# A hybrid decoder block on one core: new source for norm 1, RoPE on another engine, other orders of the split products

## The chip, the core and the metric

The kernel runs on one core of one Trainium2 chip. Its time is the device time of one execution in microseconds (us). Three runs of the kernel before took 1512.32, 1514.86 and 1514.89 us; the median is 1514.86 us. The engines are TensorE (PE in the profile; its weight loads are PEld), VectorE (DVE), ScalarE (ACT), GpSimd (POOL) and SyncE (SP), which here only issues DMAs.

## The reference

One decoder layer on x of 256 tokens x 2048 features, all in fp32. Two token mixers stand side by side and are merged by sigmoid gates; a SwiGLU FFN and a last norm follow. D_FF is 5632.

```
def rms_norm(x, w):
    y = xf * lax.rsqrt(jnp.mean(xf * xf, axis=-1, keepdims=True) + NORM_EPS)
    return (y * w.astype(jnp.float32)).astype(x.dtype)
...
def apply_rope(x, cos, sin):
    return jnp.concatenate([x1 * c - x2 * s, x2 * c + x1 * s], axis=-1).astype(x.dtype)
...
        h = rms_norm(x, norm1_w[l])
        proj = h @ w_in[l]
        nsa_q, nsa_kv, nsa_g, dn_qkv, dn_z, dn_a, dn_b, merge_g = jnp.split(proj, split_points(), axis=-1)
...
        mixed = g_nsa * (o_nsa @ w_up_nsa[l]) + g_dn * (o_dn @ w_up_dn[l])
        x = x + mixed @ w_o[l]
        h2 = rms_norm(x, norm2_w[l])
        x = x + (jax.nn.silu(h2 @ w_ffn_gate[l]) * (h2 @ w_ffn_up[l])) @ w_ffn_down[l]
    return rms_norm(x, norm_f_w)
```

## The kernel before, in words

Every weight matrix is streamed once through SBUF in tiles `raw` of 128 partitions x 2048 fp32 (1 MB; 708 KB in the first stage), three buffers deep, by SP's queue (`load`, L122). TensorE multiplies in fp32r, so each operand is cut in two parts: `split` (L133) lets ScalarE copy half a tile to `hi` (L141) and VectorE subtract it to get `lo` (L142), three buffers of each. A product of weight w and activation a is the sum of hi*hi, hi*lo and lo*hi. There are two ways to form it:

- `group` with `nat_mm` (L144, L234): the activation is the stationary operand and the weight streams, three products of up to 512 columns (L238 to L240). Used for the first stage (z, a, b and NSA gates, three groups of 354 to 356 columns, called zab), for v of NSA, for w_o and for the FFN's down projection.
- `group_t` (L180) and `group_s` (L206): the weight is stationary, the activation streams. `group_t` streams the activation's two parts at once (512 columns, L196) against w's hi, then the activation's hi (256 columns, L197) against w's lo; hi*hi and hi*lo land in two halves of a PSUM bank, which ScalarE and VectorE add afterwards (L200, L202). One such unit (weight tile k, column half f) is two products, and f is the innermost loop but the products of one unit stand together. `group_s` makes three products of 256 columns into one accumulator (L220 to L222), both f in one bank; it serves the DeltaNet's q, k and v (called wdn).

The stages follow each other on TensorE: zab, wdn (6 x 2 groups), NSA kv and q (`nsaT`) and v, merge gates (16 groups), DeltaNet's and NSA's up projections (`odn`, `onsa`), w_o, FFN gate and up (22 steps of two groups, `wfg`), FFN down. All small work of the mixers (conv, triangular solve, DeltaNet's chunk steps, RoPE, attention) is written as generators in three lanes; `pump` lets one step of each lane into the program after every half tile, so that this work lies between the products. The scheduler puts the splits some way ahead (`high_priority`), and instructions in `pin` keep their written order.

At the start, class `First` (L987) loads x transposed (`xT`), makes the hi and lo parts of x times the norm's weight (L1001, L1002), and lets GpSimd square and add the columns of `xT` (L1008, L1011, L1012). After the first group, `rms1` (L1050) sums these over the partitions by 8 fp32 products with a vector of ones (L1056, `ssx`) and takes the reciprocal root; the factor is applied when products leave PSUM. `rope` (L684) is four GpSimd instructions on each of three k tensors and four q tensors (L690 to L693): two on 64 partitions, two on 128, each of 512 elements. `solve` inverts a 32x32 triangle in 31 steps on VectorE, with a yield after most of them.

Of the kernel before, what the change touches and what calls it, by code (L numbers as in the profile page):

```python
# [14 lines left out]
P = 128  # L15
# [78 lines left out]
class Kern:  # L94
# [27 lines left out]
    def load(self, src, w, nk=4, parts=1):  # L122
# [3 lines left out]
        m = nk // parts  # L126
        for i in range(parts):
            nc.sync.dma_start(rv[:, i * m:(i + 1) * m, :], src[:, i * m:(i + 1) * m, :])
            if parts > 1:
                self.on_load(i)  # L130
        return rv

# [12 lines left out]
    def group(self, srcs, acts, w=512, first=None, t_outer=False):  # L145
# [3 lines left out]
        if t_outer:  # L149
            ps = [self.aux("mm")[:], self.aux("mm")[:]]  # L150
        else:
            bank = self.pmain.tile([P, 2, 512], F32, tag="mm", name=self.nm("mm"))
            ps = [bank[:, t, :] for t in range(2)]
        n = len(srcs)
        tail = []
        for c, src in enumerate(srcs):
            if first:
                first.load(c)
            rv = self.load(src, w, parts=2 if first and c == 0 else 1)
            for h in range(2):  # L160
                if first:
                    first.prep(c, h)
                hv, lv = self.split(rv, w, h)
# [16 lines left out]
    def group_t(self, srcs, acts, out=None):  # L180


        nc = self.nc
        ps = self.pmain.tile([P, 2, 2, 256], F32, tag="mm", name=self.nm("mm"))
        n = len(srcs)
        for c, src in enumerate(srcs):
            rv = self.load(src, 256, nk=8)
            for h in range(2):
                hv, lv = self.split(rv, 256, h)
                for k in range(4):  # L190
                    a = acts(c * 8 + h * 4 + k)
                    begin = c == 0 and h == 0 and k == 0
                    last = c == n - 1 and h == 1 and k == 3
                    for f in range(2):
                        fs = slice(f * P, f * P + P)
                        nc.tensor.matmul(ps[:, f], hv[:, k, fs], a, start=begin, stop=False, skip_group_check=True)  # L196
                        nc.tensor.matmul(ps[:, f, 0, :], lv[:, k, fs], a[:, 0, :], start=False, stop=last, skip_group_check=True)  # L197
                self.pump()
        e = self.wp.tile([P, 2, 256], F32, tag="ev", bufs=1, name=self.nm("ev"))
# [4 lines left out]

    def group_s(self, srcs, acts):

        nc = self.nc
        ps = self.pmain.tile([P, 2, 256], F32, tag="mm", name=self.nm("mm"))
        n = len(srcs)
        for c, src in enumerate(srcs):  # L210
            rv = self.load(src, 256, nk=8)
            for h in range(2):
                hv, lv = self.split(rv, 256, h)
                for k in range(4):
                    a = acts(c * 8 + h * 4 + k)
                    begin = c == 0 and h == 0 and k == 0
                    last = c == n - 1 and h == 1 and k == 3
                    for f in range(2):
                        fs = slice(f * P, f * P + P)
                        nc.tensor.matmul(ps[:, f], hv[:, k, fs], a[:, 0, :], start=begin and f == 0, stop=False, skip_group_check=True)  # L220
                        nc.tensor.matmul(ps[:, f], hv[:, k, fs], a[:, 1, :], start=False, stop=False, skip_group_check=True)  # L221
                        nc.tensor.matmul(ps[:, f], lv[:, k, fs], a[:, 0, :], start=False, stop=last, skip_group_check=True)  # L222
                self.pump()
        return ps[:]
# [202 lines left out]
    def solve(self):  # L427
# [28 lines left out]
        for q in range(4):  # L456
            self.pin(V.tensor_tensor(self.MT[:, 4 * q:4 * q + 4, :], self.MT[:, 4 * q:4 * q + 4, :],
                                     self.cs["offmask"][:, None, :].to_broadcast([P, 4, 128]), op=OP.mult))
            yield
# [3 lines left out]
        for j in range(31):  # L463
# [5 lines left out]
            if j % 2 or 7 < j < 23:  # L469
                yield  # L470
# [213 lines left out]
    def rope(self, x):  # L684

        G = self.nc.gpsimd
# [7 lines left out]
        t.free()  # L694

    def nsa_kv(self):
# [17 lines left out]
        nc.gpsimd.tensor_tensor(vc.ap, vc.ap, self.R[:, None, :].to_broadcast([P, 2, 256]), op=OP.mult)  # L714
        for x in (kc, ks, kw):
            self.rope(x)
            yield
# [68 lines left out]
    def nsa_q(self):  # L786
# [10 lines left out]
        for x in self.qT4:  # L797
            self.rope(x)
            yield
# [83 lines left out]
        def values(t, h, pt):  # L883
# [4 lines left out]
            for br in range(2):  # L888
                for kb in range(nb):
                    c = br * 256 + kvh * 128  # L890
                    nc.tensor.matmul(ov[:, j, :], self.vn[:, kb, c:c + 128], pt[:, br * nb + kb, :],  # L891
# [38 lines left out]
        self.vn.free()  # L930


    def build(self):
# [24 lines left out]
        nc.sync.dma_start(n1[:], t["n1"])  # L958

# [21 lines left out]
        acc = self.ar.alloc([4, 256], "y")  # L981
# [4 lines left out]
        class First:  # L986
# [6 lines left out]
            def part(_, h):  # L993
                nc.sync.dma_start(xT[:, 2 * h:2 * h + 2, :], t["xT"][:, 2 * h:2 * h + 2, :])

            def prep(_, c, h):
# [6 lines left out]
                if h:  # L1003
                    sq = self.ar.alloc([4, 256], "ym")
                    sqs.append(sq)
                    xc = xT[:, 4 * c:4 * c + 4, :]
                    if c < 3:
                        nc.gpsimd.tensor_tensor(sq.ap, xc, xc, op=OP.mult)  # L1008
                    else:
                        nc.scalar.activation(sq.ap, xc, AF.Square)  # L1010
# [337 lines left out]
```

## Time and profile before

| What | Value |
|---|---|
| Median of three runs | 1514.86 us |
| Profiled execution, its own time | 1514.85 us |
| Its span | 1513.1 us |
| PE busy | 1485.2 us (98%) |
| DVE, ACT, POOL busy | 971.9, 719.7, 147.6 us |
| Mean granted TensorE clock | 0.994 of 2.4 GHz |

The span runs from the first to the last instruction of the execution; 1.75 us of the execution's time lie around it. A busy PE does not say how fast it goes: its matmuls overlap, so the pace is read from starts, or from the number of matmuls in a stretch. Where PE waits, the waits and the order of time tell for whom.

### The profile page before, as it was taken

The numbers are of one execution on the slowest core, as the hardware profiler recorded it, in microseconds if no ns is written. First come the engines' busy times: TensorE is split into PE (matmuls) and PEld (weight loads), VectorE is DVE, ScalarE is ACT, GpSimd is POOL, SyncE is SP. The second block draws the span as 40 slices with busy tenths as digits, with TensorE's granted clock in tenths as the row PEclk, the third lists the DMA queues.
The fourth block names the chain that finished last, engine by engine and source line by source line (L and its number), as shares of the span: only waits on it lengthen the run. The fifth ranks groups of instructions, "written<-read, shape, count | busy, mean of one in ns | idle before, by whom it ended". The sixth has DMA issues, their size and how long they took to land.

```text
span 1513.1 us, 21295 instructions
## 1 busy us (share of the span) xinstructions
PE 1485.2 (98%) x8583; PEld 1303.0 (86%) x8583; DVE 971.9 (64%) x1400; ACT 719.7 (48%) x923; POOL 147.6 (10%) x109
## 2 busy tenths in 40 slices
PE   6999999999999999999999999999999999999997
PEld 6999998897888988888888888888888888888885
DVE  7679997668777765675665565555555555445443
ACT  5655444344455545554454444444445444333343
POOL 5000103302400000030000000000000000000000
PEclk9999999999999999999999999999999999999999
DMA  6654556345554465555455555555555556555553
GB/s 232 224 188 168 182 168 199 108 151 185 198 180 152 139 200 190 172 191 194 167 192 185 184 191 195 195 188 183 190 191 195 194 181 212 191 195 183 183 190 112
DMA packets 40947, 276.80 MB, mean 183 GB/s; under 512 B 4992, under 2 KB 5008, under 8 KB 9232
## 3 DMA queue, kind: packets, MB, share of 16 engines
q1 hardware_dynamic: 38592, 268.34, 52.3%
q10 hardware_dynamic: 1152, 4.46, 0.9%
q0 software_dynamic: 1104, 2.64, 0.7%
q8 instruction: 67, 1.10, 0.3%
q14 instruction: 32, 0.26, 0.0%
HBM read 272.52 MB, written 2.89 MB: 182 GB/s over the span
## 4 chain that ended last, share of the span: by engine, by line
PE 95%; DVE 3%; DMA 0%; issue 0%; ACT 0%; SPq 0%; DVEq 0%; ACTq 0%
PE mm L196 36%; PE mm L197 18%; PE mm L239 9%; PE mm L240 9%; PE mm L238 9%; PE mm L221 3%; PE mm L222 3%; PE mm L220 3%; DVE lo L142 1%; PE oacc L891 1%; PE U L563 1%; DMA raw<-in_zab 0%; PE pt L877 0%; DVE xs L468 0%; DVE main L376 0%
## 5 line engine op out<-in xcount | busy, mean ns | idle before, releaser
L142 DVE TENSOR_TENSOR lo<-raw,hi 128x1024 fp32r<-128x1024 f32 (+2 forms) x512 | 635.1, 1242 | 471.4 <-ACT hi L141 470.0
L141 ACT ACTIVATE hi<-raw 128x1024 fp32r<-128x1024 f32 (+2 forms) x512 | 535.6, 1047 | 728.3 <-PE mm L196 378.5
L196 PE MATMUL mm<-h,hi 128*128 128x512 f32 x1408 | 488.6, 392 | 0.0
L197 PE MATMUL mm<-h,lo 128*128 128x256 f32 x1408 | 394.6, 280 | 0.0
L196 PEld LDWEIGHTS mm<-h,hi 128*128 128x128 f32 x1408 | 264.2, 188 | 59.1
L196 PE MATMUL mm<-hh,hi 128*128 128x512 f32 x768 | 276.5, 401 | 0.0
L197 PEld LDWEIGHTS mm<-h,lo 128*128 128x128 f32 x1408 | 264.7, 188 | 0.0
L197 PE MATMUL mm<-hh,lo 128*128 128x256 f32 x768 | 217.5, 283 | 5.3 <-DVE lo L142 5.3
L196 PEld LDWEIGHTS mm<-hh,hi 128*128 128x128 f32 x768 | 145.1, 189 | 33.4 <-issue 0.2
L197 PEld LDWEIGHTS mm<-hh,lo 128*128 128x128 f32 x768 | 145.7, 190 | 7.4 <-DVE lo L142 7.2
L220 PE MATMUL mm<-hh,hi 128*128 128x256 f32 x384 | 108.7, 283 | 0.0
L221 PE MATMUL mm<-hh,hi 128*128 128x256 f32 x384 | 107.9, 281 | 0.0
L222 PE MATMUL mm<-hh,lo 128*128 128x256 f32 x384 | 107.9, 281 | 0.0
L1196 POOL TENSOR_TENSOR sgt<-sgt,R 128x512 f32<-128x512 f32 x22 | 39.6, 1802 | 536.9 <-ACT sgt L1195 536.9
L239 PE MATMUL mm<-lo,fxy 128*128 128x512 f32 x192 | 75.9, 395 | 0.0
L240 PE MATMUL mm<-hi,fxy 128*128 128x512 f32 x192 | 75.9, 395 | 0.0
L238 PE MATMUL mm<-hi,fxy 128*128 128x512 f32 x192 | 75.9, 395 | 0.0
L220 PEld LDWEIGHTS mm<-hh,hi 128*128 128x128 f32 x384 | 72.4, 188 | 0.0
L221 PEld LDWEIGHTS mm<-hh,hi 128*128 128x128 f32 x384 | 72.4, 189 | 0.0
L222 PEld LDWEIGHTS mm<-hh,lo 128*128 128x128 f32 x384 | 72.4, 188 | 0.0
L239 PE MATMUL mm<-lo,fa 128*128 128x512 f32 x160 | 63.2, 395 | 0.0
L238 PE MATMUL mm<-hi,fa 128*128 128x512 f32 x160 | 63.2, 395 | 0.0
(351 smaller groups left out, 1885.8 us busy)
## 6 DMA issues: line engine op xcount, KB each, us to landing
raw<-in_wfg SPq DMA_DIRECT2D x88, 1024.0 KB, 4.8
raw<-in_wd SPq DMA_DIRECT2D x44, 1024.0 KB, 4.8
raw<-in_wmg SPq DMA_DIRECT2D x32, 1024.0 KB, 4.8
raw<-in_wdn SPq DMA_DIRECT2D x24, 1024.0 KB, 4.9
raw<-in_nsa SPq DMA_DIRECT2D x16, 1024.0 KB, 4.8
raw<-in_wo SPq DMA_DIRECT2D x16, 1024.0 KB, 4.8
raw<-in_wud SPq DMA_DIRECT2D x8, 1024.0 KB, 4.9
raw<-in_wun SPq DMA_DIRECT2D x8, 1024.0 KB, 4.8
```

Source lines behind the costliest of these rows:

```text
L141: nc.scalar.activation(hv, rv[:, m * h:m * h + m, :], AF.Copy)
L142: nc.vector.tensor_tensor(lv, rv[:, m * h:m * h + m, :], hv.bitcast(F32), op=OP.subtract)
L196: nc.tensor.matmul(ps[:, f], hv[:, k, fs], a, start=begin, stop=False, skip_group_check=True)
L197: nc.tensor.matmul(ps[:, f, 0, :], lv[:, k, fs], a[:, 0, :], start=False, stop=last, skip_group_check=True)
L220: nc.tensor.matmul(ps[:, f], hv[:, k, fs], a[:, 0, :], start=begin and f == 0, stop=False, skip_group_check=True)
L221: nc.tensor.matmul(ps[:, f], hv[:, k, fs], a[:, 1, :], start=False, stop=False, skip_group_check=True)
L222: nc.tensor.matmul(ps[:, f], lv[:, k, fs], a[:, 0, :], start=False, stop=last, skip_group_check=True)
L238: nc.tensor.matmul(o, a[:, 0, sl], hv[:, k, :], start=begin, stop=False)
L239: nc.tensor.matmul(o, a[:, 0, sl], lv[:, k, :], start=False, stop=False)
L240: nc.tensor.matmul(o, a[:, 1, sl], hv[:, k, :], start=False, stop=last)
L563: nc.tensor.matmul(bv[:, j, :], Pm[t, hg][:, j, :], U[t, hg][:, j, :], start=True, stop=True)
L1196: nc.gpsimd.tensor_tensor(sgt[:], sgt[:], self.R2b, op=OP.mult)
```

## The change

- Start: nine products of 128 columns with a tensor of ones go to TensorE before the first real one (`idle`). The first weight chunk is loaded in pieces (1, 1 and 2 of its four k tiles), the first two by ScalarE's queue; `split_one` splits it k by k, and the activation's hi part of that chunk is made by VectorE. The first group accumulates in two of the three auxiliary PSUM banks.
- Norm 1: x is loaded once more in rows (`xn`, two DMAs of 1 MB on SP's queue behind the first chunk of the second group), and ScalarE squares and sums it in four instructions of 1024 elements. GpSimd's squares and sums and the 8 products `ssx` are gone.
- RoPE: the same four instructions on VectorE, with a yield after each two; the scaling of v_c by R moves to VectorE too.
- `group_t` takes an order. `w`, its default, puts both f of the hi product ahead of both f of the lo product, in other words alternates PSUM banks product by product; it now holds for NSA, merge gates and up projections. `s` is the DeltaNet's three narrow products with f innermost and each f in its own bank. In the FFN's gate and up the orders w, w1, w2, w3, s, s1, s2 take turns by step: 13 of 22 steps stay wide, 9 become narrow.
- `solve` yields in fewer places; the NSA v tile becomes two tiles.

```diff
-            rv = self.load(src, w, parts=2 if first and c == 0 else 1)
+            rv = self.load(src, w, parts=[(0, 1), (1, 2), (2, 4)] if first and c == 0 else None)
...
+                self.on_load(k0, k1)
+                (nc.scalar if i < 2 else nc.sync).dma_start(rv[:, k0:k1, :], src[:, k0:k1, :])
...
+    def split_one(self, rv, w, h, ahead):
...
+            for k in range(2):
+                self.pin(nc.scalar.activation(hv[:, k, :], rv[:, 2 * h + k, :], AF.Copy))
+                ahead(2 * h + k)
+                self.pin(nc.vector.tensor_tensor(lv[:, k, :], rv[:, 2 * h + k, :], hv[:, k, :].bitcast(F32), op=OP.subtract))
...
-    def group_t(self, srcs, acts, out=None):
+    def group_t(self, srcs, acts, out=None, order="w"):
...
+        acc = [ps[:, f, 0, :] for f in range(2)] if order != "s2" else [ps[:, 0, f, :] for f in range(2)]
+        both, K = range(2), range(4)
+        if wide:
+            seq = {"w": [(k, f, p) for k in K for p in both for f in both],
+                   "w1": [(k, f ^ p, p) for k in K for p in both for f in both],
+                   "w2": [(2 * j + k, f, p) for j in both for p in both for k in both for f in both],
+                   "w3": [(k, f, p) for p in both for f in both for k in K]}[order]
+        else:
+            seq = {"s": [(k, f, p) for k in K for p in range(3) for f in both],
+                   "s1": [(k, f, p) for p in range(3) for k in K for f in both],
+                   "s2": [(k, f, p) for k in K for p in range(3) for f in both]}[order]
...
+                    if wide and p == 0:
+                        nc.tensor.matmul(ps[:, f], hv[:, k, fs], a, **kw)
+                    elif wide:
+                        nc.tensor.matmul(ps[:, f, 0, :], lv[:, k, fs], a[:, 0, :], **kw)
+                    else:
+                        nc.tensor.matmul(acc[f], (hv, hv, lv)[p][:, k, fs], a[:, p % 2, :], **kw)
...
-            if j % 2 or 7 < j < 23:
+            if j % 2 or 10 < j < 20:
...
-        G.tensor_tensor(t[lo], x[hi], s[hi], op=OP.mult)
-        G.tensor_tensor(t[hi], x[lo], s[lo], op=OP.mult)
-        G.tensor_tensor(x.ap, x.ap, c, op=OP.mult)
-        G.tensor_tensor(x.ap, x.ap, t.ap, op=OP.add)
+        self.pin(V.tensor_tensor(t[lo], x[hi], s[hi], op=OP.mult))
+        self.pin(V.tensor_tensor(t[hi], x[lo], s[lo], op=OP.mult))
+        yield
+        self.pin(V.tensor_tensor(x.ap, x.ap, c, op=OP.mult))
+        self.pin(V.tensor_tensor(x.ap, x.ap, t.ap, op=OP.add))
...
+        idle = self.aux("idle")
+        for _ in range(9):
+            self.pin(nc.tensor.matmul(idle[:, :128], self.ones[:, 0:1].to_broadcast([P, P]), self.ones[:, 1:2].to_broadcast([P, P]), start=True, stop=True))
...
-                if h:
-                    sq = self.ar.alloc([4, 256], "ym")
...
-                        nc.gpsimd.tensor_tensor(sq.ap, xc, xc, op=OP.mult)
...
+            for tt in range(2):
+                self.pin(nc.sync.dma_start(xn[:, tt, :], t["x"][:, tt, :]))
...
+                for i in range(2):
+                    q = xn[:, tt, i * 1024:i * 1024 + 1024]
+                    self.pin(nc.scalar.activation(q, q, AF.Square, accum_out=ssx[:, tt, i:i + 1]))
+                    yield
...
-                e = self.group_s([t["wdn"][(g * 2 + half) * 2 + c] for c in range(2)], hact)
+                e = self.group_t([t["wdn"][(g * 2 + half) * 2 + c] for c in range(2)], hact, order="s")
...
+            order = ["w", "w1", "w2", "w3", "s", "s1", "s2"][g % 7]
-            e = self.group_t([t["wfg"][g * 4 + c] for c in range(2)], h2)
+            e = self.group_t([t["wfg"][g * 4 + c] for c in range(2)], h2, order=order)
```

The first products on PE, before (`mm` is the PSUM tile, `hi` and `lo` the weight's parts, `hh` the activation's):

```order
L1344 UNCONDITIONAL_BRANCH
L238 MATMUL mm_102<-hi_112,hh_95 128x354
L239 MATMUL mm_102<-lo_113,hh_95 128x354
L240 MATMUL mm_102<-hi_112,hh_95 128x354
L238 MATMUL mm_102<-hi_112,hh_95 128x354
```

The first products on PE now (`idle` is the bank that takes the products of ones):

```order
L1372 UNCONDITIONAL_BRANCH
L987 MATMUL idle_86<-ones 128x128 x9
L260 MATMUL mm_113<-hi_122,hh_106 128x354
L260 MATMUL mm_114<-hi_122,hh_106 128x354
L261 MATMUL mm_113<-lo_123,hh_106 128x354
L262 MATMUL mm_113<-hi_122,hh_106 128x354
```

Nine products stand ahead of the first real one, and the two products of the hi parts come before the first that needs `lo`.

RoPE of two of the q tensors, before on POOL (`main` is the arena that holds them, `consts` the tables):

```order
L690 TENSOR_TENSOR main<-main,consts 64x512
L691 TENSOR_TENSOR main<-main,consts 64x512
L692 TENSOR_TENSOR main<-main,consts 128x512
L693 TENSOR_TENSOR main<-main 128x512
L690 TENSOR_TENSOR main<-main,consts 64x512
L691 TENSOR_TENSOR main<-main,consts 64x512
```

The same now on DVE, among the splits (`lo`) and the sums of a merge gate's products (`ev`):

```order
L713 TENSOR_TENSOR main<-main,consts 64x512
L714 TENSOR_TENSOR main<-main,consts 64x512
L158 TENSOR_TENSOR lo_4234<-raw_4209,hi_4233 128x1024
L716 TENSOR_TENSOR main<-main,consts 128x512
L717 TENSOR_TENSOR main<-main 128x512
L158 TENSOR_TENSOR lo_4258<-raw_4255,hi_4257 128x1024
L713 TENSOR_TENSOR main<-main,consts 64x512
L714 TENSOR_TENSOR main<-main,consts 64x512
L245 TENSOR_TENSOR ev_4204<-mm_4102,ev_4204 128x512
```

Two RoPE instructions now stand between two splits, eight times in a row; POOL has none.

An up projection on PE, before (`odn` is the activation):

```order
L196 MATMUL mm_5796<-odn,hi_5799 128x512
L197 MATMUL mm_5796<-odn,lo_5800 128x256
L196 MATMUL mm_5796<-odn,hi_5799 128x512
L197 MATMUL mm_5796<-odn,lo_5800 128x256
L196 MATMUL mm_5796<-odn,hi_5799 128x512
```

The same place now, and behind the line of dots a narrow step of the FFN (`h` is the FFN's activation):

```order
L234 MATMUL mm_5801<-odn,hi_5804 128x512 x2
L236 MATMUL mm_5801<-odn,lo_5805 128x256 x2
L234 MATMUL mm_5801<-odn,hi_5804 128x512 x2
L236 MATMUL mm_5801<-odn,lo_5805 128x256 x2
...
L238 MATMUL mm_8007<-h_6602,hi_8010 128x256 x4
L238 MATMUL mm_8007<-h_6602,lo_8011 128x256 x2
L238 MATMUL mm_8007<-h_6602,hi_8010 128x256 x4
L238 MATMUL mm_8007<-h_6602,lo_8011 128x256 x2
```

Products of 512 columns now follow each other in twos (in fours and eights in the orders w2 and w3), where a 512 and a 256 alternated; a narrow step is 256 columns throughout.

## Rows read from the trace of the kernel before

**Rows 1.** Page: busy us (share) and instructions of each engine
```profile
PE 1485.2 (98%) x8583; PEld 1303.0 (86%) x8583; DVE 971.9 (64%) x1400; ACT 719.7 (48%) x923; POOL 147.6 (10%) x109
```
**Rows 2.** Stretches: length, busy us (rows) of PE PEld DVE ACT POOL, clock, DMA
```profile
5.90:33.30 27.40, 20.64 (x96) 19.53 (x97) 25.03 (x26) 14.15 (x26) 16.65 (x13) 0.88 0.67 252
...
19.50:24.10 4.60, 4.54 (x15) 4.54 (x16) 4.60 (x7) 0.89 (x2) 2.71 (x4) 0.50 0.29 79
24.10:33.30 9.20, 9.20 (x57) 9.20 (x57) 7.43 (x10) 5.63 (x10) 2.67 (x2) 0.99 0.54 191
33.30:67.90 34.60, 34.41 (x218) 33.88 (x217) 21.16 (x57) 20.30 (x27) 2.89 (x5) 1.00 0.58 195
...
371.10:382.50 11.40, 6.96 (x31) 5.53 (x30) 11.40 (x8) 2.21 (x3) 10.66 (x8) 0.85 0.23 75
```
**Rows 3.** Groups by line, DVE, 5 to 8.4 us
```profile
L142 DVE TENSOR_TENSOR lo<-raw,hi 128x708 fp32r<-128x708 f32 x2 | 1.8, 898 | 4.9 <-ACT hi L141 4.9
L1002 DVE SCALAR_TENSOR_TENSOR hh<-xs,n1t,hh 128x256 fp32r<-128x256 f32 x2 | 0.9, 479 | 0.0
```
**Rows 4.** Groups by line, DVE and then POOL, 8 to 21.6 us
```profile
L1002 DVE SCALAR_TENSOR_TENSOR hh<-xs,n1t,hh 128x256 fp32r<-128x256 f32 x7 | 9.3, 1382 | 0.3 <-ACT hh L1001 0.3
L142 DVE TENSOR_TENSOR lo<-raw,hi 128x708 fp32r<-128x708 f32 x2 | 4.7, 2390 | 0.0
...
L1008 POOL TENSOR_TENSOR ys<-xs 128x1024 f32<-128x1024 f32 x3 | 6.0, 2010 | 3.9 <-DMA xs<-in_xT 3.9
```
**Rows 5.** DMA, first 60 us: GB/s in 40 slices of 1.5 us
```profile
GB/s 0 96 339 314 328 387 407 422 414 427 421 345 15 0 0 223 261 91 381 11 45 321 166 283 162 95 353 38 186 300 5 46 315 125 53 262 188 0 104 366
```
**Rows 6.** Chain of waits in order of time: start us, us, what
```profile
41.28 1.68 PE ssx L1056 x16
```
**Rows 7.** Timeline around 372 us: start us, us, instruction, idle before
```profile
366.90 0.34 DVE L665 SCALAR_TENSOR_TENSOR xs<-xs,ro_y,main 128x128 f32<-128x128 f32 x1
...
371.50 2.15 POOL L693 TENSOR_TENSOR main<-main 128x512 f32<-128x512 f32 x1
372.43 5.41 DVE L665 SCALAR_TENSOR_TENSOR main<-main,ro_y 128x128 f32<-128x128 f32 x4
372.56 0.38 PE L197 MATMUL mm<-hh,lo 128*128 128x256 f32 x1 [1.05 <-DVE lo L142]
...
379.02 0.46 PE L197 MATMUL mm<-hh,lo 128*128 128x256 f32 x1 [3.38 <-DVE lo L142]
```
**Rows 8.** Stretch of PE alone: length, busy us (rows), clock, DMA
```profile
228.00:252.00 24.00, 23.14 (x137) 1.00 0.63 187
```
**Rows 9.** Groups by line, whole span, DVE
```profile
L202 DVE TENSOR_TENSOR ev<-mm,ev 128x512 f32<-128x512 f32 x76 | 51.9, 683 | 0.0
```
**Rows 10.** Stretch of DVE alone: length, busy us (rows), clock, DMA
```profile
214.00:255.00 41.00, 38.35 (x73) 1.00 0.61 191
```
**Rows 11.** Stretches of one product form each: wdn, up projections, FFN gate/up, down
```profile
100.00:108.00 8.00, 8.00 (x70) 8.00 (x69) 4.37 (x4) 3.19 (x4) 0.00 (x0) 1.00 0.48 154
590.00:670.00 80.00, 80.00 (x455) 69.45 (x454) 55.39 (x61) 47.20 (x62) 11.91 (x6) 1.00 0.55 186
800.00:1250.00 450.00, 450.00 (x2598) 395.55 (x2597) 263.91 (x265) 213.81 (x245) 36.52 (x20) 1.00 0.56 190
1300.00:1480.00 180.00, 180.00 (x773) 144.65 (x772) 84.89 (x77) 72.84 (x79) 9.21 (x6) 1.00 0.56 187
```
**Rows 12.** Timeline, PE, in the up projections
```profile
599.75 0.40 PE L196 MATMUL mm<-odn,hi 128*128 128x512 f32 x1
599.99 0.28 PE L197 MATMUL mm<-odn,lo 128*128 128x256 f32 x1
600.11 0.39 PE L196 MATMUL mm<-odn,hi 128*128 128x512 f32 x1
600.34 0.28 PE L197 MATMUL mm<-odn,lo 128*128 128x256 f32 x1
```

More of the change, by code (lines that the diff above doesn't have):

```diff
@@ L119, in drain, with load @@
             self.pump()
-    def load(self, src, w, nk=4, parts=1):
+    def load(self, src, w, nk=4, parts=None):
         nc = self.nc
@@ L189, in group_t @@
                 hv, lv = self.split(rv, 256, h)
-                for k in range(4):
+                for i, (k, f, p) in enumerate(seq):
                     a = acts(c * 8 + h * 4 + k)
[L192 to L197, printed above, removed]
+                    fs = slice(f * P, f * P + P)
+                    bank = 0 if order == "s2" else f
+                    begin = bank not in seen
+                    seen.add(bank)
+                    last = c == n - 1 and h == 1 and all(g != f for _, g, _ in seq[i + 1:])
+                    kw = dict(start=begin, stop=last, skip_group_check=True)
+                    if wide and p == 0:
+                        nc.tensor.matmul(ps[:, f], hv[:, k, fs], a, **kw)
+                    elif wide:
+                        nc.tensor.matmul(ps[:, f, 0, :], lv[:, k, fs], a[:, 0, :], **kw)
+                    else:
+                        nc.tensor.matmul(acc[f], (hv, hv, lv)[p][:, k, fs], a[:, p % 2, :], **kw)
                 self.pump()
+        if not wide:
+            return ps[:, 0] if order == "s2" else ps[:, :, 0, :]
         e = self.wp.tile([P, 2, 256], F32, tag="ev", bufs=1, name=self.nm("ev"))
@@ L203, in group_t @@
         return out
[L205 to L224, printed above, removed]
     def hilo(self, out, v):
@@ L797, in nsa_q @@
         for x in self.qT4:
-            self.rope(x)
-            yield
+            yield from self.rope(x)
         yield
@@ L929, in nsa_q @@
                 yield
-        self.vn.free()
+        for v in self.vn:
+            v.free()
     def build(self):
@@ L1050, in rms1 @@
         def rms1(ps):
-            for _ in range(3):
+            for tt in range(2):
+                self.pin(nc.sync.dma_start(xn[:, tt, :], t["x"][:, tt, :]))
+            for _ in range(2):
                 yield
-            bank = self.aux("ssx")
             for tt in range(2):
-                for i in range(4):
-                    self.pin(nc.tensor.matmul(bank[:, tt:tt + 1], acc[:, i, tt * P:(tt + 1) * P], self.ones[:, 0:1],
-                                              start=tt == 0 and i == 0, stop=i == 3, skip_group_check=True))
-            v = norm_factor(bank[:, 0:2], "r1")
+                for i in range(2):
+                    q = xn[:, tt, i * 1024:i * 1024 + 1024]
+                    self.pin(nc.scalar.activation(q, q, AF.Square, accum_out=ssx[:, tt, i:i + 1]))
+                    yield
+            ss = self.small([2], "ssx1")
+            V.tensor_reduce(ss[:], ssx[:], axis=AX.X, op=OP.add)
+            v = norm_factor(ss[:], "r1")
             V.tensor_copy(rstd1[:], v[:])
             xT.free()
-            acc.free()
-            for sq in sqs:
-                sq.free()
+            xn.free()
             evac_zab(0, ps)
@@ L1196, in build @@
             nc.gpsimd.tensor_tensor(sgt[:], sgt[:], self.R2b, op=OP.mult)
-            e = self.group_t([t["wfg"][g * 4 + 2 + c] for c in range(2)], h2)
+            e = self.group_t([t["wfg"][g * 4 + 2 + c] for c in range(2)], h2, order=order)
             V.tensor_tensor(sgt[:], e, sgt[:], op=OP.mult)
```

65 lines of the change are left out of this document (37 added, 28 removed).

## The prediction

> **What bounds the kernel.** I read the page's busy times first, then the stretches and groups of the start, then the chain and the timelines, then one stretch per form of product. TensorE is busy for 1485.2 of 1513.1 us [rows 1], so time can come from two places only: stretches in which it waits or runs slowly, and the time between two of its products where it never waits. The reader should see the first in three places. From the first product at 5.90 us to the end of the first group at 33.30 us there are 96 products in 27.4 us, while the 57 that end the group take 9.20 us, 161 ns each [rows 2]; at that pace 96 would take 15.5, so 11.9 us are lost. From 371.1 to 382.5 us, 11.4 us hold 31 products [rows 2], and by 176.6 ns (below) they need 5.5: some 5.9 lost. From 228 to 252 us PE idles for 0.86 us [rows 8]. Everywhere else it goes like a metronome at granted clock 1.00, the upper level of 2.4 GHz [rows 11].
>
> For the second kind I divide a stretch by its products, less two rows that overlap its edges [rows 11]. The three 256-column products of a DeltaNet unit: 8.00/68 = 117.6 ns each, 352.9 a unit. A wide unit (512 and 256 columns) in the up projections: 80/453 = 176.6, 353.2 a unit. The same in the FFN: 450/2596 = 173.3, 346.7 a unit. 512 columns after 512 (down): 180/771 = 233.5. So the same wide unit costs 6.5 ns more in one stage than in another. In the up projections the starts show it: from one 512 to its 256 it is 0.24 us, the next time 0.23 [rows 12].
>
> **Start.** PE waits there for VectorE, and VectorE is slow. Ahead of GpSimd's squares a `lo` of 708 columns takes 898 ns and a part of `hh` 479 [rows 3]; beside GpSimd's squares of 2010 ns they take 2390 and 1382 [rows 4]. The change takes the squares and sums away. VectorE's need for the first group is then eight `lo` at 898, sixteen parts of `hh` at 479 and four hi parts of the first chunk (taken at 479 as well): 7.2 + 7.7 + 1.9 = 16.8 us. It starts at about 5 us, where the first piece lands, so it ends near 22; the last products follow it by some 0.5 us: 22.5 in place of 33.3, a gain of 10.8. Bounds: the floor of TensorE, 15.5 us from about 5.3, would end at 20.8 (gain 12.5). If the products still run at the pace of the lower clock, 15 in 4.60 us or 307 ns at granted clock 0.50 (the level of 1.2 GHz, after PE had waited) [rows 2], for about a third of the group, the end is 22.5 + 32 x 0.146 = 27.2 (gain 6.1). The nine products of ones fill PE before its first real one, where it now stands still. The data don't bind: some 4.9 MB (x in columns and four weight chunks) at about 400 GB/s are in after 12 us, by about 15 us of the span [rows 5]. The 2 MB of rows of x come behind; they take 5 us of SP's queue when the second group needs 2.8 MB in 15.5 us, 180 GB/s, which leaves room. ScalarE's four squares of 1024 elements lie beside products (it is busy 20.30 of 34.60 us there [rows 2]). What waits for them is only the factor of norm 1, used when a group leaves PSUM. I take −10.8.
>
> The `ssx` products go: 1.68 us on the chain [rows 6], −1.7.
>
> **RoPE.** From 371 to 382 us VectorE's `xs` takes 1.35 us each (5.41 for four) beside GpSimd's RoPE against 0.34 alone, `lo` is late, and PE waits 1.05 and 3.38 us for it [rows 7]. With GpSimd out, VectorE has the work itself: four instructions of 512 elements, at 683 ns each (the nearest row of that length [rows 9]), 2.7 us a tensor, 19.1 for seven, and 0.7 for v_c. Two stand between two splits. A half tile lasts 16 products of 176.6 = 2.83 us; a split's `lo` of 1024 at about 1.25 us (898 x 1024/708, rounded down), and 1.37 of RoPE, and now and then a sum at 0.68: 2.6 to 3.3 us. That is just full, with three buffers of `lo` ahead to even it out. Best: all of the loss goes, −5.9 and −0.9 more by 252 us; worst: each of the 14 pairs brings the overrun of 0.5 us, and nothing is gained. I take −5.5, near the best, because pairs with a sum are the fewer. From 214 to 255 us VectorE is busy 38.35 of 41.00 us [rows 10], and `solve` yields in fewer places there, so its runs between two splits get longer. I count neither gain nor loss there, between −0.9 and +3 (six yields fewer, 0.5 us each).
>
> **Orders of the products.** In order w two units are 512, 512, 256, 256. By rows: 233.5 for a 512 after a 512, the FFN's 346.7 − 117.6 = 229.1 for the other, 2 x 117.6: 697.8, 348.9 a unit. Against 353.2 that would be −4.3 on 1024 units of NSA, gates and up projections, −4.4 us. If the surplus of 6.5 ns a unit that the up projections have over the FFN [rows 11] stays as it is, they cost 355.4 and it is +2.3. I take −2, nearer the first, which is put together from rows. In the FFN orders w and w1 (7 steps of 64 units, 448) cost 348.9 against 346.7: +1.0. Orders w2 (four 512s, four 256s; 350.0 a unit) and w3 (eight and eight; 350.5) on 192 units each: +0.6, +0.7. Narrow orders on 9 steps, 576 units, at 352.9: 576 x 6.2 ns = +3.6. FFN together +5.9. The DeltaNet keeps its form and only turns banks at each product: 0. That the turn costs or gives nothing is my choice: no row has a stage that turns banks at every product, and rivals 1 and 4 are its bounds.
>
> "Perfetto Trace Analysis", Optimizing Tensor Performance, of the Trainium skill says that larger matmuls are more efficient than smaller ones where possible. That speaks against the narrow steps, and the rows agree: 352.9 against 346.7 for the same arithmetic. "TensorE: Matmul & The Clock Gate", LDWEIGHTS, of the Trainium skill prices a weight load by columns at 1.2 GHz, 107 ns for 128 as an estimate; as the floor of a narrow product it would make 576 units 14.8 us cheaper than now. No row here is that fast: the narrow products take 117.6.
>
> **Sum.** −10.8 − 1.7 − 5.5 − 2.0 + 5.9 = −14.1. The profiled execution took 1514.85 us, 0.01 from the median: 1500.7 us. Of products, 1856 units of two and 960 of three get a new order, 6592, so 2.1 ns each is worth the whole gain.
>
> **Rivals.**
> 1. *Banks in turn make products faster.* If a product that writes another bank than the one before need not wait for it, a 256 could take half of a 512, 229.1/2 = 114.5 ns, and every unit 343.6: the narrow FFN steps 576 x −3.1 = −1.8 in place of +3.6, DeltaNet 384 x −9.3 = −3.6, the units before the FFN 1024 x −9.6 = −9.8 in place of −2, wide FFN steps 832 x −3.1 = −2.6 in place of +2.3. That is 21.7 less, 1479. For it: banks are what most of the new orders turn. Against it: 512 columns after 512 in one bank go at 233.5, only 2% more. 0.08.
> 2. *VectorE becomes the bound.* The RoPE pairs and the longer runs of `solve` make `lo` late: the −5.5 is lost, and +3 by 250 us, 1509.2. For it: 38.35 of 41.00 us [rows 10]. Against it: two instructions at a time are about what a half tile has room for. 0.12.
> 3. *The start is bound elsewhere.* Lower clock or late pieces let the first group end at 27.2, 4.7 later than I say, 1505.4; with waits behind the 2 MB of rows of x, some 1508. 0.14.
> 4. *Slower.* If half the units carry the 6.5 ns a unit between up projections and FFN, each of these carries 13; rows 12 show the two kinds in turn. An order that puts products of a kind together may put every unit on the dear side: wide FFN 832 x 13 = +10.8, narrow 576 x 13 = +7.5, DeltaNet 384 x 13 = +5.0, the units before the FFN 1024 x (348.9 + 13 − 353.2) = +8.9. With +5.9 and −18.0 from start, `ssx` and RoPE: +20.1, 1535. It decides from 2.1 ns a product. For it: the surplus is there in the up projections [rows 11], and nothing in the rows explains it. Against it: the FFN, the longest stage, has the same products without it. 0.09.
>
> My forecast keeps 0.57. Its own range is 1494 (the start at its floor, RoPE at its best, FFN half as dear) to 1506. With rivals 2 and 3 the range is 1487 to 1511, which leaves rivals 1 and 4 and some 0.03 outside. A measurement tells 0.2%, 3 us, from no change. Faster than 1511.8: the forecast and rivals 1 to 3 but for 0.05 of these, 0.86. Same: 0.06, that part and a little of the way to rival 4. Slower: 0.08.
>
> **What would show it.** The first group ends near 22.5 us and `lo` of 708 columns stays near 0.9 us; no `ssx`; RoPE's instructions on VectorE take about 0.68 us; no PE wait over 1 us near 372 us. Wide units of NSA and up projections at 349 ns, FFN steps at 349, 349, 350, 350 and 353 for narrow. I am wrong if the narrow steps leave 353 by more than 5 ns, if PE waits for `lo` beside RoPE, or if SP's queue is late for the second group.

## The result, and the profile after

The changed kernel takes 1497.29 us (median of four runs, 1496.0 to 1498.47), the kernel before 1514.03 (four runs). The ratio is 0.9891, with a 95% interval of 0.9873 to 0.9908: 1.1% faster. The forecast was 1500.7, with 1487 to 1511 as range. The profiled executions differ by 18.35 us (1514.85 and 1496.50), their spans by 18.4. Later executions of the kernel before fall into two groups, 1511.7 to 1516.3 and 1522.9 to 1525.2 us; the four here belong to the first, and the experiments below are set against the changed kernel or compared stage by stage.

The page's busy line of the changed kernel, which answers to [rows 1]:

```profile
PE 1478.1 (99%) x9161; PEld 1324.0 (89%) x9161; DVE 948.9 (63%) x1418; ACT 714.9 (48%) x910; POOL 82.6 (6%) x69
```

GpSimd lost 65 us of work and VectorE is 23 us less busy than before, although it took over RoPE. The starts of the products on TensorE say where the time went. The table has the time in us at which each stretch ends, before and after (the start of the next stretch's first product; in the last row the end of the span), and by how much the stretch itself got longer or shorter:

| Stretch | Ends, before | Ends, after | Change | Forecast |
|---|---|---|---|---|
| to the end of the first group | 33.31 | 24.41 | −8.9 | −10.8 |
| groups 2 and 3, to wdn | 67.94 | 59.46 | +0.4 | −1.7 |
| wdn, to NSA | 213.98 | 205.67 | +0.2 | 0 |
| NSA and merge gates, to the up projections | 584.20 | 564.69 | −11.2 | −5.5 (RoPE), −1.5 (order) |
| up projections, to w_o | 674.65 | 653.45 | −1.7 | −0.5 |
| w_o | 767.09 | 745.89 | 0.0 | 0 |
| FFN gate and up, to down | 1256.78 | 1238.80 | +3.2 | +5.9 |
| to the end of the span | 1513.07 | 1494.65 | −0.4 | 0 |

*The start.* Three stretches of the changed kernel, with the columns of [rows 2], and VectorE's groups from 8 to 21 us, which answer to [rows 4]:

```profile
4.75:24.41 19.66, 17.66 (x99) 15.76 (x98) 15.98 (x31) 11.88 (x23) 1.10 (x2) 1.00 1.00 398
24.41:33.30 8.89, 7.29 (x44) 6.75 (x43) 2.60 (x3) 4.57 (x8) 0.00 (x0) 1.00 0.71 265
...
356.80:367.00 10.20, 10.20 (x67) 9.18 (x65) 6.23 (x7) 5.39 (x7) 0.00 (x0) 1.00 0.67 244
```

```profile
L158 DVE TENSOR_TENSOR lo<-raw,hi 128x708 fp32r<-128x708 f32 x6 | 5.2, 890 | 0.6 <-ACT hi L157 0.6
L1037 DVE SCALAR_TENSOR_TENSOR hh<-xs,n1t,hh 128x256 fp32r<-128x256 f32 x12 | 5.0, 480 | 0.0
```

`lo` takes 890 ns and a part of `hh` 480 through the whole group. The DMA share is 1.00 in that stretch, and until 12.9 us PE waits three times for data: the chain of waits there runs from a piece of x in columns, landing at 9.40 us, over ScalarE's parts of `hh` and `hi` to `lo`:

```profile
3.06 6.34 DMA xs<-in_xT
...
9.49 1.71 ACT hh L1036 x4
11.20 0.73 ACT hi L157
...
11.95 0.72 DVE lo L158
```

The DMA line of the first 60 us (40 slices of 1.5 us) shows it full until 28.5 us, against 18 us in [rows 5]:

```profile
GB/s 0 188 342 243 321 388 398 431 409 428 416 414 441 439 399 437 405 415 423 287 34 72 376 38 106 365 68 330 125 209 277 0 87 306 360 218 410 251 415 55
```

In the second group PE waits twice, 1.10 us before its product at 29.58 us and 0.50 us before that at 30.51. The chain of waits names a weight chunk that was issued at 16.88 us and took 11.74 us to land:

```profile
16.88 11.74 DMA raw<-in_zab
```

*The middle.* The 48 products from number 2064 on took 15.93 us before (367.31 to 383.24, the stall of [rows 7]) and take 10.21 now, PE without a gap (the third stretch above): −5.7. RoPE's instructions take the forecast time on VectorE:

```profile
L717 DVE TENSOR_TENSOR main<-main 128x512 f32<-128x512 f32 x4 | 2.8, 688 | 0.1
L713 DVE TENSOR_TENSOR main<-main,consts 64x512 f32<-64x512 f32 x4 | 2.7, 686 | 0.1
```

*The pace.* Stretches of PE alone, columns as in [rows 8]: wdn, the up projections, narrow FFN steps, a step in order w, and the steps w2 and w3 together. They answer to [rows 11] (products less two):

```profile
62.00:102.00 40.00, 40.00 (x345) 1.00 0.63 224
568.00:608.00 40.00, 40.00 (x233) 1.00 0.53 186
840.00:900.00 60.00, 60.00 (x516) 1.00 0.54 181
904.00:926.00 22.00, 22.00 (x129) 1.00 0.56 191
...
792.00:836.00 44.00, 44.00 (x252) 1.00 0.55 192
```

wdn 40/343 = 116.6 ns a product, up projections 40/231 = 173.2 (176.6 before), narrow FFN 60/514 = 116.7, w 22/127 = 173.2, w2 and w3 44/250 = 176.0. By the starts of whole steps (the first step apart), which have no edges, a unit costs 346.7 in w and w1, 349.8 in w2, 350.0 in w3 and 350.0 in s, s1 and s2 alike.

In wdn the 8 us of [rows 11] were too short for the pace of before. A longer stretch of the kernel before gives 36/304 = 118.4 ns a product, and by the starts of half tiles without other work a unit took 355.0 ns before and takes 350.0 now:

```profile
68.00:104.00 36.00, 36.00 (x306) 1.00 0.64 211
```

On 384 units that is 1.9 us less, yet the stretch is 0.2 us longer. PE now waits there for small work of the DeltaNet: 0.81 us for a transpose of v (`vtr`) and 0.72 for one of q (`qtr`), with 0.88 more for `qtr` in the next stretch; before it had no such waits. The first line is of the changed kernel, the second of the kernel before with only the solve's yields changed (below), so the `qtr` waits come with the fewer yields:

```profile
PE qtr L531 <- ACT main L402: 1.6, 2, 0.9
PE qtr L509 <- ACT main L380: 2.1, 2, 1.2
```

### The profile page after: what moved, and what is told of

The parts are those of the page before. It is cut to its first block, busy times and chain, and to the rows that moved or that the text cites. A ratio compares the mean times of both kernels' runs of the same rounds, so it can differ in the third digit from the quotient of the medians.

```text
span 1494.6 us, 22412 instructions
## 1 busy us (share of the span) xinstructions
PE 1478.1 (99%) x9161; PEld 1324.0 (89%) x9161; DVE 948.9 (63%) x1418; ACT 714.9 (48%) x910; POOL 82.6 (6%) x69
## 4 chain that ended last, share of the span: by engine, by line
PE 94%; DVE 3%; DMA 1%; ACT 1%; issue 0%; SPq 0%; DVEq 0%; ACTq 0%
PE mm L234 28%; PE mm L238 22%; PE mm L236 14%; PE mm L261 8%; PE mm L262 8%; PE mm L260 8%; DVE lo L158 1%; DMA raw<-in_zab 1%; PE oacc L916 1%; PE U L586 1%; DMA xs<-in_xT 0%; PE pt L902 0%; DVE xs L491 0%; DVE main L398 0%; DVE xs L489 0%
## 5 line engine op out<-in xcount | busy, mean ns | idle before, releaser
L234 PE MATMUL mm<-hh,hi 128*128 128x512 f32 x768 | 241.0, 395 | 0.0
L234 PE MATMUL mm<-h,hi 128*128 128x512 f32 x832 | 240.3, 393 | 0.0
L236 PEld LDWEIGHTS mm<-hh,lo 128*128 128x128 f32 x768 | 144.1, 188 | 32.0
L238 PE MATMUL mm<-h,hi 128*128 128x256 f32 x1152 | 169.2, 279 | 0.0
L236 PEld LDWEIGHTS mm<-h,lo 128*128 128x128 f32 x832 | 139.0, 188 | 25.2
L236 PE MATMUL mm<-hh,lo 128*128 128x256 f32 x768 | 153.3, 281 | 0.0
L238 PEld LDWEIGHTS mm<-h,hi 128*128 128x128 f32 x1152 | 149.6, 188 | 0.0
L236 PE MATMUL mm<-h,lo 128*128 128x256 f32 x832 | 145.7, 280 | 0.0
L234 PEld LDWEIGHTS mm<-h,hi 128*128 128x128 f32 x832 | 135.8, 188 | 11.0
L238 PE MATMUL mm<-hh,hi 128*128 128x256 f32 x768 | 121.9, 280 | 0.0
L234 PEld LDWEIGHTS mm<-hh,hi 128*128 128x128 f32 x768 | 118.0, 188 | 0.3 <-issue 0.2
L238 PEld LDWEIGHTS mm<-hh,hi 128*128 128x128 f32 x768 | 103.3, 188 | 0.0
L238 PE MATMUL mm<-h,lo 128*128 128x256 f32 x576 | 102.0, 279 | 0.0
L238 PEld LDWEIGHTS mm<-h,lo 128*128 128x128 f32 x576 | 82.4, 188 | 0.0
L238 PE MATMUL mm<-hh,lo 128*128 128x256 f32 x384 | 76.0, 279 | 0.0
```

What stands on the lines that cost most here:

```text
L234: nc.tensor.matmul(ps[:, f], hv[:, k, fs], a, **kw)
L236: nc.tensor.matmul(ps[:, f, 0, :], lv[:, k, fs], a[:, 0, :], **kw)
L238: nc.tensor.matmul(acc[f], (hv, hv, lv)[p][:, k, fs], a[:, p % 2, :], **kw)
```

## The experiments

### GpSimd's squares put back

```diff
+                nc.gpsimd.tensor_tensor(sq.ap, xc, xc, op=OP.mult)
+                nc.gpsimd.tensor_tensor(sq[:, 0:2, :], sq[:, 0:2, :], sq[:, 2:4, :], op=OP.add)
+                nc.gpsimd.tensor_tensor(sq[:, 0, :], sq[:, 0, :], sq[:, 1, :], op=OP.add)
```

> The changed kernel, with GpSimd's squares and adds of the columns of x put back as extra work (their result is not used; norm 1 still comes from the rows). Theory (GpSimd's squares slow VectorE's two-input instructions, and this held up the first group): a lo of 708 columns goes from 0.85 us back to 2 us and more while a square runs, the first group of 96 products ends at 28 to 33 us in place of 24.4, and the time rises by 4 to 9 us. Rival (the pieces, the products of ones or the banks brought the gain): the first group still ends before 25.5 us, the time rises by less than 1 us.

Measured: 1504.21 us (1504.01 to 1504.67), +6.9. The first group ends at 34.46 us. Its stretch, and VectorE's and GpSimd's groups from 8 to 21 us:

```profile
4.75:34.46 29.71, 21.10 (x99) 18.95 (x98) 24.82 (x31) 12.22 (x24) 13.39 (x11) 0.77 0.83 313
```

```profile
L1029 DVE SCALAR_TENSOR_TENSOR hh<-xs,n1t,hh 128x256 fp32r<-128x256 f32 x2 | 4.1, 2032 | 0.1
L146 DVE TENSOR_TENSOR lo<-raw,hi 128x354 fp32r<-128x354 f32 x2 | 3.2, 1582 | 0.0
...
L1045 POOL TENSOR_TENSOR main<-xs 128x1024 f32<-128x1024 f32 x3 | 5.9, 1967 | 2.6 <-DMA xs<-in_xT 2.4
```

The `lo` of 354 columns takes 1582 ns in place of 526, a part of `hh` 2032 in place of 486, and TensorE's mean granted clock in that stretch is 0.77, with waits in it, in place of 1.00. The two lines of the changed kernel to set beside these:

```profile
L146 DVE TENSOR_TENSOR lo<-raw,hi 128x354 fp32r<-128x354 f32 x2 | 1.1, 526 | 0.8 <-ACT hi L144 0.8
L1029 DVE SCALAR_TENSOR_TENSOR hh<-xs,n1t,hh 128x256 fp32r<-128x256 f32 x1 | 0.5, 486 | 0.0
```

With GpSimd's work alone back, pieces, leading products and rows of x in place, the first group ends as late as in the traces of the kernel before and its variants (33.31 to 34.99). So the squares account for the whole 8.9 us: while they run, none of the other changes brings the group's end forward. Products 96 to 288 then take 32.93 us in place of 35.05, so wdn begins 7.9 us later and not 10.

### No leading products

```diff
-        for _ in range(9):
+        for _ in range(0):
```

> The changed kernel without the nine products of ones at the start. Theory A (they matter for the clock): the first products run at granted clock 0.50, some 300 ns each in place of 161, until PE has been busy for some time; up to 20 of them, so the first group ends up to 3 us later. Theory B (PE waits for data until 13.5 us anyway): the clock is low, but the first group ends within 0.7 us of 24.4 and the time is the same within 1 us.

Measured: 1496.37 us (1495.44 to 1498.38), the same. The first group ends at 24.24. The two timelines, without them and then with them (start us, us, instruction, idle before):

```profile
6.32 0.50 PE L262 MATMUL mm<-hi,hh 128*128 128x354 f32 x1
6.61 0.50 PE L261 MATMUL mm<-lo,hh 128*128 128x354 f32 x1
6.91 0.50 PE L262 MATMUL mm<-hi,hh 128*128 128x354 f32 x1
```

```profile
5.77 0.32 PE L262 MATMUL mm<-hi,hh 128*128 128x354 f32 x1
5.93 0.33 PE L261 MATMUL mm<-lo,hh 128*128 128x354 f32 x1
6.10 0.33 PE L262 MATMUL mm<-hi,hh 128*128 128x354 f32 x1
```

Starts 0.29 to 0.30 us apart against 0.16 to 0.17: the products of ones do lift the first real ones to the faster pace. It gains nothing, as theory B had it: PE waits for `hi` and `lo` behind them in either case, until 12.7 us without them and 12.9 with them.

### The first chunk in two halves

```diff
-            rv = self.load(src, w, parts=[(0, 1), (1, 2), (2, 4)] if first and c == 0 else None)
+            rv = self.load(src, w, parts=[(0, 2), (2, 4)] if first and c == 0 else None)
...
-                (nc.scalar if i < 2 else nc.sync).dma_start(rv[:, k0:k1, :], src[:, k0:k1, :])
+                nc.sync.dma_start(rv[:, k0:k1, :], src[:, k0:k1, :])
```

> The changed kernel with the first weight chunk loaded in two halves (two k tiles each) on SP's queue, as before, in place of pieces of one, one and two tiles with the first two on ScalarE's queue. The splits stay k by k. Theory: the first product starts some 1 us later than 4.75, but the later chunks are bound by the DMA, so the first group ends at most 0.7 us later than 24.4. Rival (the pieces bring the start forward): the first group ends over 1 us later and the time rises by as much.

Measured: 1497.34 us (1496.3 to 1498.46), the same. The first product starts at 6.00 in place of 4.75, the group ends at 24.61 in place of 24.41. The earlier start is lost to the later waits, which end at 13.1 us here and at 12.9 there.

### The second megabyte of rows one chunk later

```diff
-            for tt in range(2):
-                self.pin(nc.sync.dma_start(xn[:, tt, :], t["x"][:, tt, :]))
+            self.pin(nc.sync.dma_start(xn[:, 0, :], t["x"][:, 0, :]))
             for _ in range(2):
                 yield
+            self.pin(nc.sync.dma_start(xn[:, 1, :], t["x"][:, 1, :]))
```

> The changed kernel with the second megabyte of the rows of x issued one weight chunk later. Theory (PE's waits of 1.43 and 0.93 us between products at 28.15 and 29.58 us come from a weight chunk that stands in SP's queue behind the 2 MB of rows): both waits go and products 96 to 288 take 33 us in place of 35.05; the time falls by 1.5 to 2 us. Rival (ScalarE's four squares of rows hold up the hi parts there): the waits stay or move to the later place of the squares, and the time is the same within 0.7 us.

Measured: 1495.11 us (1494.41 to 1495.95), 2.2 less. The stretch from 27 to 31 us, without the edit (the changed kernel) and with it:

```profile
27.00:31.00 4.00, 2.40 (x14) 1.86 (x13) 1.44 (x2) 2.27 (x3) 0.00 (x0) 1.00 0.67 276
```

```profile
27.00:31.00 4.00, 4.00 (x26) 3.79 (x25) 1.71 (x2) 3.37 (x7) 0.00 (x0) 1.00 0.85 306
```

PE is busy throughout, and products 96 to 288 take 33.33 us in place of 35.05. The waits were for the weight chunk behind the rows. So the `ssx` products did go, and a DMA took their place.

### RoPE back on GpSimd, in the changed kernel

```diff
-        V = self.nc.vector
+        V = self.nc.gpsimd
```

> The changed kernel with RoPE's four instructions on GpSimd again (the yields of the new version stay). Theory: the stall of the kernel before returns where the q tensors get RoPE, VectorE's lo goes from 1.2 to 2 us and more, PE waits some 4 to 6 us in all, and the time rises by 4 to 7 us. Rival (the gain between 200 and 585 us comes from the order of the products alone): the time rises by less than 1 us.

Measured: 1498.02 us (1497.38 to 1500.03), +0.7. By the trace, products 2016 to 2064 take 1.4 us longer and nothing else changes in the middle. The theory fell: RoPE on GpSimd is not enough for the stall. The next two go from the kernel before.

### The kernel before with only RoPE and its yields changed

```diff
-        G = self.nc.gpsimd
+        G = self.nc.vector
...
+        yield
```

> The kernel before, with RoPE on VectorE and its yields as in the changed kernel, and nothing else. RoPE on GpSimd cost the changed kernel only 1.4 us, so the stall of the kernel before, 5.7 us between its products 2064 and 2112, may have another cause or need a second one. Theory P (the stall needs GpSimd's RoPE and VectorE's scaling of the DeltaNet's output, L665, at one time; either change takes them apart): the stall goes, these 48 products take 9 to 11 us in place of 15.9. Theory S (the stall is VectorE's own load there, whoever does RoPE): it stays at 4 us or more.

Measured: one execution of 1516.75 us, with an FFN 9.1 us slower than in the profile of before (see the pace, below). The same 48 products (from number 2064 on) take 9.43 us in place of 15.93. Here the scaling of the DeltaNet's output, L665, has its own time again (1.13 us for four, 5.41 in [rows 7]):

```profile
369.80 1.13 DVE L665 SCALAR_TENSOR_TENSOR main<-main,ro_y 128x128 f32<-128x128 f32 x4
```

### The kernel before with only the solve's yields changed

```diff
-            if j % 2 or 7 < j < 23:
+            if j % 2 or 10 < j < 20:
```

> The kernel before, with the fewer yields of the triangular solve as in the changed kernel, and RoPE still on GpSimd. Theory P (the stall of 5.7 us between products 2064 and 2112 needs GpSimd's RoPE beside the scaling of the DeltaNet's output on VectorE, and the shorter solve lets the DeltaNet's lane come to that point earlier than RoPE of the q tensors): the two no longer meet and the stall falls to under 2 us. Rival (any RoPE in a run of four on GpSimd holds up VectorE enough): it stays at 4 us or more.

(Of the yields between the masks' four steps half are gone too.) Measured: one execution of 1509.23 us. The same 48 products take 9.46 us, with GpSimd at RoPE beside them for 9.13 of 9.50 us and no gap on PE:

```profile
371.50:381.00 9.50, 9.50 (x59) 8.39 (x58) 9.08 (x7) 4.17 (x4) 9.13 (x6) 1.00 0.73 282
```

VectorE has 7 instructions there, slow ones; the experiment before this one has 14 in its stretch, with GpSimd idle:

```profile
367.40:376.90 9.50, 9.50 (x59) 8.39 (x58) 7.00 (x14) 4.15 (x4) 0.00 (x0) 1.00 0.73 262
```

The scaling of the DeltaNet's output (L666 in this kernel) is done before GpSimd's first RoPE of q begins:

```profile
356.76 0.34 DVE L666 SCALAR_TENSOR_TENSOR main<-main,ro_y 128x128 f32<-128x128 f32 x1
357.25 1.29 POOL L691 TENSOR_TENSOR main<-main,consts 64x512 f32<-64x512 f32 x1 [55.05 <-DVE main L666]
```

Theory P holds: the stall needs GpSimd's RoPE and the run of two-input work of the DeltaNet on VectorE at one time. Moving either apart removes it; the change did both, so its two edits don't add. What no run separates is how much of the first of these two experiments is RoPE's engine and how much the yields that came with it.

### Order w in the whole FFN

```diff
-            order = ["w", "w1", "w2", "w3", "s", "s1", "s2"][g % 7]
+            order = "w"
```

> The changed kernel with order w in all 22 steps of the FFN's gate and up. By the paces of the steps in the trace after (w and w1 346.7 ns a unit, w2 349.8, w3 350.0, narrow 350.0): 192 x 3.1 + 192 x 3.3 + 576 x 3.3 = 3.1 us less, the FFN in 489.8 us in place of 492.9. Rival (mixed forms cost something at each turn from one to the other, or the pace of w moves with its place in the program): not 346.7 in every step.

Measured: 1492.81 us (1492.38 to 1493.98), 4.5 less; by the trace the FFN takes 489.54 us, 3.4 less. The paces of the steps had given 3.1; the other 1.1 us of the median's 4.5 lie outside the FFN and are not explained.

### Other forms in the FFN

```diff
-            order = ["w", "w1", "w2", "w3", "s", "s1", "s2"][g % 7]
+            order = ["wo", "w", "so", "so2", "s", "w3"][g % 6]
```

> The changed kernel, with other forms in the FFN's 22 steps, taking turns: the old wide order (the 512 and the 256 of a unit together), w, the DeltaNet's old narrow order (the three products of a unit together) with each f in its own bank, the same with both f in one bank, s, w3. Theory 1 (a unit's price depends on the order and on where its weight loads fall in PE's instructions, counted by eights): the old wide order, which went at 346.7 in the FFN before, goes at 353 here, since the count of PE's instructions ahead of it is another by an odd number; w stays at 346.7; the old narrow order goes at 352 to 355 with either choice of banks, s at 350.0. Theory 2 (banks in turn): the old narrow order with two banks differs from that with one. Theory 3 (the stage sets the price): the old wide order goes at 346.7 as in the FFN before.

Measured: one execution of 1497.49 us. A step of the old wide order, and of the old narrow order with two banks:

```profile
883.00:904.00 21.00, 21.00 (x123) 1.00 0.56 196
928.00:949.00 21.00, 21.00 (x182) 1.00 0.55 197
```

21/121 = 173.6 and 21/180 = 116.7 ns; by whole steps (the first apart) 346.8 a unit for the old wide order and 346.9 for w, 350.0 for the old narrow order with two banks, with one, and for s. In this execution theory 1 and theory 2 fail: neither the order within a unit nor the banks change the price. Theory 3, that the stage does, fits this run, but not the next two.

### One more product ahead of the up projections of the kernel before

```diff
         self.drain()
+        idle = self.aux("idle")
+        self.pin(nc.tensor.matmul(idle[:, :128], hh[0][:, 0, 0, :128], hh[0][:, 0, 0, :128], start=True, stop=True))
```

> The kernel before, with one product of 128 columns more on TensorE ahead of the up projections (its result is not used). It and its weight load move every later PE instruction by two places. Theory (the 6.5 ns between the up projections and the FFN hang on the place of the weight loads in the count of PE's instructions by eights): the two swap, the up projections go at 346.7 a unit (1.7 us less for 256 units) and the FFN at 353 from its second step on (some 1340 units x 6.5 = 8.7 us more); the kernel takes 7 us more. Rival (the price belongs to the stage, its tiles or their places in memory): both keep their pace, and the time is the same within 0.5 us.

Measured: median 1514.85 us, the same as before, but of ten executions eight took 1514.1 to 1515.4 and two 1523.6 and 1524.5. The profiled one is of the second kind. Its FFN, and for comparison that of the kernel before with the solve's yields:

```profile
800.00:1250.00 450.00, 450.00 (x2549) 1.00 0.55 186
```

```profile
800.00:1240.00 440.00, 440.00 (x2540) 1.00 0.56 190
```

450/2547 = 176.7 and 440/2538 = 173.4 ns: the same products at two paces, 353.3 and 346.8 a unit, the FFN 498.8 and 489.7 us long. The up projections did not swap: 45.3 and 45.2 us, as in the kernel before; with the solve's yields alone they took 44.4 each, the better pace, in the kernel before. My count by eights is not shown, and neither is its rival. The two groups of times are 9 us apart, as far as the FFN at its two paces; the kernel before has the same two groups. So one program seems to have both paces, in different executions, though only one of the ten was traced.

The changed kernel has the dear pace too, and in order w. Its FFN begins with it: ten pairs of units from 750.35 to 757.42 us take 353.5 ns a unit. Then come four small products of norm 2 (`R`), and the next ten pairs, from 759.98 to 766.91, take 346.5:

```profile
750.35 0.63 PE L234 MATMUL mm<-h,hi 128*128 128x512 f32 x2
...
757.42 0.64 PE L234 MATMUL mm<-h,hi 128*128 128x512 f32 x2
...
758.13 0.60 PE L1053 MATMUL R<-consts,r_y 128*128 128x128 f32 x4
...
759.98 0.62 PE L234 MATMUL mm<-h,hi 128*128 128x512 f32 x2
...
766.91 0.62 PE L234 MATMUL mm<-h,hi 128*128 128x512 f32 x2
```

At the same four products the kernel before goes from 353.3 to 346.7 as well; in the traced execution of this experiment the FFN stays at 353.3 behind them.

### The old wide order in all stages of the changed kernel

```diff
-    def group_t(self, srcs, acts, out=None, order="w"):
+    def group_t(self, srcs, acts, out=None, order="wo"):
```

(and in all steps of the FFN.)

> The changed kernel with the old order (the 512 and the 256 of a unit together) in all wide stages and in all 22 steps of the FFN. Theory (the old order has two paces, 346.7 and 353.3 ns a unit, which hold for a whole stage and may differ from one execution to the next; order w has one): the executions fall into groups several us apart, between 1493 (every stage at 346.7) and 1493 + 2432 units x 6.6 ns = 1509 us, and some stage of the profile shows 353. Rival (the two paces belong to the program before alone): all executions within 3 us of each other and all stages at 346.7, some 1493 us.

Measured: 1491.84 us, five runs from 1491.41 to 1492.08 and one of 1495.03. Every stage of its trace goes at the better pace, the up projections at 44.4 us each, the FFN at 489.5. The rival was right on the trace; the one execution of 1495.03 lies 3.6 us above the lowest and has no trace. Order w is not needed to bring the up projections from 353.2 to 346.7: the old order has that pace here too.

### The best of these

Order w in the FFN and the second megabyte later, both edits as above.

> The changed kernel with order w in all steps of the FFN and the second megabyte of the rows of x one weight chunk later. If the two gains (3.4 and 2.1 us by the traces) add: 1497.0 - 5.5 = 1491.5 us, and, since w has one pace, all executions within 3 us of each other. If the earlier start of the second group only moves a wait to a later place: 1493 to 1494.

Measured: 1490.95 us (six runs, 1490.46 to 1491.46), 6.3 under the changed kernel and 23.1 under the kernel before (1514.03). The FFN takes 489.7, wdn begins at 57.80 in place of 59.46.

## Why the prediction was right, and where its terms were off

1. *GpSimd's squares hold up the start*: right, and shown by putting them back. The term was 1.9 us too large. The step that failed is "The data don't bind": I counted 4.9 MB at 400 GB/s and set them against 15 us, but piece by piece PE waited for data and what hangs on them until 12.9 us, and neither the pieces nor the leading products changed the end.
2. *`ssx` gone, −1.7*: they went, but the stretch grew by 0.4. Rival 3 named the place, "waits behind the 2 MB of rows of x", and held for about 2 us; and of my own signs of being wrong one came true, "if SP's queue is late for the second group". My count of 180 GB/s was an average over the group; the one chunk issued behind the rows took 11.74 us to land, and 1.7 us came back when half of the rows were issued behind it.
3. *RoPE, −5.5*: the stall went, −5.7. The size was right and the reason half right: the overlap with one run of VectorE's work made it, and fewer yields in the solve alone took it away too. "That is just full" for VectorE was too dark (it is busy 6.23 of 10.20 us in that stretch); rival 2 did not occur. For the solve's fewer yields I counted nothing. They took away waits for `lo` of 0.86 us before 252 us, and brought waits for `qtr` of 1.6 us.
4. *Orders before the FFN, −2*: 1024 units at 346.7 in place of 353.2 are −6.7 us (−1.7 of it measured in the up projections, the rest worked out), the largest miss. I treated the 6.5 ns as a property of the order. The run with the old order in the changed kernel shows that it is none. What sets it stays open: the old order and order w each show both paces, so does the FFN as a stage, and the pace can change within a stage. That no stage of the changed kernel or of its variants kept the dear pace for long is an observation, not an explanation, and so this part of the gain can't be credited to any one edit. The DeltaNet's 0 came out (+0.2) by luck: its units got 1.9 us cheaper, and waits ate it.
5. *FFN +5.9*: the sign was right, the size +3.2. w2 and w3 came as worked out (349.8 and 350.0 against 350.0 and 350.5); w was 346.7 and not 348.9, and the narrow product 116.7 and not 117.6. The 117.6 was read from too short a stretch; wdn before went at its dear pace, 118.3 by half tiles, which the changed kernel does not have there.
6. *Rival 1 (banks)*: out. Steps s and s2 differ in banks alone and both take 22.40 us. *Rival 4 (a dearer pace)*: the pace exists, worth 9 us in the FFN, and at it the two kinds do stand in turn (361 and 346 ns a unit by the starts in the up projections before). But it held for stages of the kernel before, and in the changed one only for short stretches.

The start brought 1.9 and 2.1 us less than the terms said, the orders 4.7 before the FFN and 2.7 in it more: the median came out 3.4 us under the forecast by errors that partly cancel.

On point 1, the Trainium skill, "SBUF — State Buffer", Who interferes with whom, says that a VectorE instruction with two SBUF inputs contends with a GpSimd instruction that reads SBUF. The traces agree: `lo` takes 526 ns without GpSimd's squares and 1582 with them, a part of `hh` 486 and 2032. The advice of the Trainium skill to prefer larger products where possible ("Perfetto Trace Analysis", Optimizing Tensor Performance) holds here by 350.0 against 346.7 ns a unit.

## What to carry to other kernels

Before moving work between GpSimd and VectorE, list what VectorE does with two inputs at that moment; the meeting decides, not the sum of busy time, and shifting one of the two by a few steps can do as much as moving the work. When a stall on one engine is removed at the start, ask at once what the DMA queue holds ahead of the next chunk. A pace that differs between stages of one kernel may not belong to the form of the products: try the old form in the new kernel before crediting a new order with it.

## What was not expected of the hardware

The 512 and 256 column products have two steady paces, 346.7 and 353.3 ns a unit, each held over a whole stage of up to 490 us at granted clock 1.00, and one program showed executions some 9 us apart. The pace can change within a stage, where a few other products stand between (353.5 to 346.5 ns at 758 us of the changed kernel). Narrow products have two paces as well: 355.0 a unit in wdn of the kernel before, 350.0 in the changed kernel and its variants, there for five orders and on one bank or two, 116.7 ns for 256 columns, half of the 233.3 of 512.
